# First head's projection ahead of half of the values, rotary tables by transposes, and a planner with other durations and a shared port

## The chip, the core and the metric

The kernel runs on one core of a Trainium2 chip. The engines are TensorE (PE, with its weight loads shown as PEld), VectorE (DVE), ScalarE (ACT), GpSimd (POOL) and SyncE (SP, which issues most DMAs). The metric is the device time of one execution in microseconds; lower is better.

## What is computed

Two layers of a decoder on 512 tokens of width 1024. Each layer has a mixing part with two groups of heads, an output projection, and a SwiGLU FFN, with RMS norms before and after both parts.

```python
for l in range(DEPTH):                      # DEPTH = 2
    h = rms_norm(x, attn_pre_g[l])
    qa, ka, va, qb, kb, vb, f_logit = jnp.split(h @ w_in[l], split_at, axis=-1)
    qa = partial_rotary(qa.reshape(b, s, 2 * N_HEADS_DIFF, HEAD_DIM), cos, sin)
    ka = partial_rotary(ka.reshape(b, s, 2 * N_HEADS_DIFF, HEAD_DIM), cos, sin)
    ...
    oa = diff_attention(qa, ka, va, lam)    # 4 heads, softmax 0 minus lam times softmax 1
    oa = rms_norm(oa, diff_sub_g[l]) * (1.0 - lam_init)
    ob = forgetting_attention(qb, kb, vb, log_sigmoid(f_logit + forget_bias[l]))   # 8 heads
    x = x + rms_norm(jnp.concatenate([oa, ob], -1) @ w_out[l], attn_post_g[l])
    h = rms_norm(x, ffn_pre_g[l])
    y = (jax.nn.silu(h @ w_gate[l]) * (h @ w_up[l])) @ w_down[l]
    x = x + rms_norm(y, ffn_post_g[l])
```

The rotary part turns the first 16 of each head's 64 columns by angles position times frequency.

## The kernel before, in words

Activations lie transposed (`hT_h`, `hT_l`: 128 columns by 8 blocks by 512 tokens). Every fp32 product is made of three matmuls: each operand is split into a rounded part and a rest (`_h` or `wh`, written by ACT; `_l` or `wl`, the difference, written by DVE or POOL), and high times high, high times low and low times high are summed in PSUM.

The attention part of a layer is not written in its order. Functions (`start`, `tables`, `tile_chunk`, `v_chunks`, `diff_head`, `fox_head`, `o0_chunk`, `o1_chunks`) add operations to a `Plan`: engine, a duration in ns (from `dV`, `dA`, `dG` of the number of columns, or a constant), operations that it depends on, a key (lower goes first among those that are ready) and the buffers that it takes and gives. `Plan.run` walks through planned time and emits each engine's instructions in the order that comes out; that order is then fixed, and on the chip each engine executes its own list and waits on semaphores. Operations with a key from `FILLER` on are fillers: PE takes them when nothing else is ready by the plan.

In layer 0, `start` loads x and the weights of the diff heads' values (`w_load`, 4 chunks `c`), normalizes the four blocks of 128 tokens, transposes them (`hp_a`), and makes the values `va` (4 token blocks `t` by 4 chunks, 6 matmuls each). Matmuls on zeros (from `sinT`) keep PE busy until then. `tables` makes the rotary tables: SP loads the positions eight times, DVE reduces 32 angles per partition, ACT takes the sines, and the tables go through DRAM (`tab_d`) into `cosT` and `sinT`. It also loads the mask, the matrix of ones (`tu`, cast into `upr`) and the small parameters (`lv`, `fbb`, `dsg`). Then fillers follow each other: key and query projections of a pair of heads (`pj_kd`, `pj_qd`, `pj_kf`, `pj_qf`, 24 matmuls each), values of the other group (`vb`), output projection (`o`). A diff head needs rotated queries and keys (`t1`, `t2` on DVE, then splits), scores (`sd`), softmax on DVE and ACT (`ed`; L958 is the combination of the two softmaxes), transposes (`ptd`) and its product with the values (`od`). A fox head has a bias made by POOL, scores `sf`, softmax (`ae`; L1037 scales by the row sums), transposes `ptf` and the product `of`. Weights of most projections are split with the rest on POOL (`wl_` in L649).

In layer 1 the values are made at the end of layer 0's FFN, and its plan starts at the key projection. The FFN is outside the plan.

## Time and profile before

| | us |
|---|---|
| runs of the kernel before | 1246.26 median of 3 (1244.06 to 1253.99) |
| profiled execution | 1249.71 |
| its span in the trace | 1247.9, mean granted clock 0.993 |
| PE busy in the span | 1201.7 (96%) |
| DVE, ACT, POOL busy | 817.3 (65%), 599.2 (48%), 210.4 (17%) |

The profiled execution is 3.45 us above the median, and 1.8 us of it lie around the span. A busy PE is not PE at its peak: a matmul's record runs on after the next has started, so short gaps between matmuls do not show as idle time.

### The profile page before, as it was taken

Reading aid. Unit: us, or ns where it says so; the run is one execution under the profiler, and the core shown is the slowest. Engines: PE = TensorE matmul, PEld = TensorE weight load, DVE = VectorE, ACT = ScalarE, POOL = GpSimd, SP = SyncE. Lnnn points to the kernel's source line nnn. Section 1 sums busy time; section 2 is a strip of 40 time slices with the busy share of each in tenths; the row PEclk is TensorE's granted clock in tenths of the full one; section 3 lists DMA queues with packets and bytes.
Section 4 is the critical chain, followed back from the end, with each engine's and each line's share of the span. In section 5 each row is a group of like instructions: output and inputs, shape, how many; then the busy total and the mean of one; then the engine's idle time right before and its main releaser. Section 6 shows DMA issues by size and latency. Waiting matters only on the chain.

```text
span 1247.9 us, 16724 instructions
## 1 busy us (share of the span) xinstructions
PE 1201.7 (96%) x5817; PEld 989.3 (79%) x5817; DVE 817.3 (65%) x1574; ACT 599.2 (48%) x1162; POOL 210.4 (17%) x250
## 2 busy tenths in 40 slices
PE   8999999999999999999799999999999999999996
PEld 5787877788888888887687878777988888887875
DVE  7697858665554545576848977695755455555855
ACT  5476757553333233365544767674533233324643
POOL 1302457320000000000223124572200000000001
PEclk9999999999999999999999999999999999999999
DMA  7333443416575766798504333434167676677863
GB/s 231 91 85 93 112 115 105 136 37 196 188 238 182 227 203 211 251 313 264 171 2 119 90 89 93 121 110 125 62 192 242 196 214 212 208 233 247 294 203 125
DMA packets 211268, 206.75 MB, mean 166 GB/s; under 512 B 11680, under 2 KB 155680, under 8 KB 211184
## 3 DMA queue, kind: packets, MB, share of 16 engines
q1 hardware_dynamic: 211040, 205.16, 53.2%
q8 instruction: 46, 0.75, 0.3%
q10 hardware_dynamic: 144, 0.52, 0.1%
q14 instruction: 38, 0.31, 0.1%
HBM read 163.34 MB, written 33.91 MB: 158 GB/s over the span
## 4 chain that ended last, share of the span: by engine, by line
PE 44%; issue 32%; DVE 13%; ACT 4%; DMA 4%; POOL 2%; SPq 0%; POOLq 0%; DVEq 0%; ACTq 0%
PE pj_g L205 10%; PE pj_u L205 10%; PE o L205 4%; PE va L205 3%; PE pj_kf L205 2%; PE pj_kd L205 2%; PE da L205 2%; PE pj_qf L205 2%; DMA rs<-s_d 2%; PE vb L205 1%; DVE t2kd L739 1%; PE db L205 1%; PE ptf L210 1%; DVE ed L958 1%; PE of L205 1%
## 5 line engine op out<-in xcount | busy, mean ns | idle before, releaser
L205 PE MATMUL pj_g<-hT_h,wh_g 128*128 128x512 f32 (+1 forms) x384 | 142.9, 372 | 0.0
L205 PE MATMUL pj_g<-hT_l,wh_g 128*128 128x512 f32 (+1 forms) x384 | 142.6, 371 | 0.0
L205 PE MATMUL pj_g<-hT_h,wl_g 128*128 128x512 f32 (+1 forms) x384 | 142.6, 371 | 0.0
L205 PE MATMUL pj_u<-hT_h,wh_u 128*128 128x512 f32 (+1 forms) x368 | 140.1, 381 | 0.0
L205 PE MATMUL pj_u<-hT_l,wh_u 128*128 128x512 f32 (+1 forms) x368 | 139.8, 380 | 0.0
L205 PE MATMUL pj_u<-hT_h,wl_u 128*128 128x512 f32 (+1 forms) x368 | 139.8, 380 | 0.0
L271 POOL TENSOR_SCALAR v_fp<-s_fp 128x1 f32<-128x1 f32 x8 | 5.2, 651 | 685.4 <-ACT junk L277 354.7
L259 DVE TENSOR_TENSOR wl_u<-wr_u,wh_u 128x1024 fp32r<-128x1024 f32 x44 | 53.9, 1225 | 98.5 <-ACT wh_u L258 98.5
L258 ACT CAST wh_g<-wr_g 128x1024 fp32r<-128x1024 f32 x44 | 46.4, 1054 | 145.9 <-PE pj_u L205 86.9
L205 PE MATMUL da<-wh_d,op 128*128 128x512 f32 x352 | 111.3, 392 | 2.1 <-ACT wh_d L258 2.1
L258 ACT CAST wh_u<-wr_u 128x1024 fp32r<-128x1024 f32 x44 | 46.3, 1053 | 135.4 <-PE pj_g L205 128.3
L1239 DVE TENSOR_TENSOR sg<-pj_u,sg 128x512 f32<-128x512 f32 x44 | 30.4, 690 | 80.8 <-PE pj_u L205 80.8
L205 PEld LDWEIGHTS pj_g<-hT_h,wh_g 128*128 128x128 f32 x384 | 72.4, 188 | 12.7
L205 PEld LDWEIGHTS pj_g<-hT_h,wl_g 128*128 128x128 f32 x384 | 72.2, 188 | 12.5
L205 PEld LDWEIGHTS pj_g<-hT_l,wh_g 128*128 128x128 f32 x384 | 72.3, 188 | 12.3
L205 PE MATMUL da<-wl_d,op 128*128 128x512 f32 x176 | 69.7, 396 | 10.9 <-DVE wl_d L259 10.9
L205 PEld LDWEIGHTS pj_u<-hT_h,wl_u 128*128 128x128 f32 x368 | 69.2, 188 | 13.2
L205 PEld LDWEIGHTS pj_u<-hT_h,wh_u 128*128 128x128 f32 x368 | 69.2, 188 | 13.1
L205 PEld LDWEIGHTS pj_u<-hT_l,wh_u 128*128 128x128 f32 x368 | 69.2, 188 | 12.9
L205 PEld LDWEIGHTS da<-wh_d,op 128*128 128x128 f32 x352 | 66.4, 189 | 16.4 <-ACT wh_d L258 2.9
L258 ACT CAST wh_d<-wr_d 128x1024 fp32r<-128x1024 f32 x42 | 44.2, 1052 | 42.4 <-PE da L205 15.4
L259 DVE TENSOR_TENSOR wl_d<-wr_d,wh_d 128x1024 fp32r<-128x1024 f32 x42 | 51.3, 1222 | 19.2 <-ACT wh_d L258 18.6
(301 smaller groups left out, 3019.1 us busy)
## 6 DMA issues: line engine op xcount, KB each, us to landing
wr_g<-in_w_gate_dram SPq DMA_DIRECT2D x44, 512.0 KB, 4.4
wr_u<-in_w_up_dram SPq DMA_DIRECT2D x44, 512.0 KB, 4.6
b<-in_w_down_dram SPq DMA_DIRECT2D x88, 256.0 KB, 3.6
t_d<-b SPq DMA_DIRECT2D x88, 256.0 KB, 4.0
wr_d<-t_d SPq DMA_DIRECT2D x24, 512.0 KB, 4.9
wr_d<-in_w_down_dram SPq DMA_DIRECT2D x18, 512.0 KB, 5.0
wr_o<-in_w_out_dram SPq DMA_DIRECT2D x16, 512.0 KB, 4.4
xr<-t_d SPq DMA_DIRECT2D x16, 512.0 KB, 5.1
```

The costliest lines, as they stand in the source:

```text
L205: ins = PE.matmul(out, a, b, start=start, stop=stop)
L210: ins = PE.transpose(out, a, idn)
L258: A.copy(hi, raw)
L259: (eng or V).tensor_sub(lo, raw, hi.bitcast(F32))
L271: G.tensor_scalar(v, s2[:, 0:1], scalar1=s2[:, 1:2], scalar2=EPS, op0=ALU.add, op1=ALU.add)
L739: return V.tensor_mul(b["t2"], b["t2"], sinT)
L958: return V.scalar_tensor_tensor(e0, e0, b["r"][:, 0:1], e1, op0=ALU.mult, op1=ALU.add)
L1239: V.tensor_mul(sg, pu, sg)
```

## The change

Six things are edited, all in the attention part.

1. In layer 0 the values of token blocks 2 and 3 get a filler's key (`VA_EARLY` = 2), and the first diff head's key and query projections a key ahead of them. For this, the value weights get other buffers, so that those of keys and queries are free.
2. The rotary tables: one DMA from ACT's queue loads the positions as 128 partitions by 4 elements; DVE makes angles for 8 frequencies and reduces them, in `start`, with a key near those of the norms; ACT writes sines and cosines into two tiles of 128 tokens by 4 blocks; PE transposes these, and ACT copies the results into `cosT` and `sinT`. The way through DRAM is gone. ACT loads the table set for sines first of all.
3. The planner's durations: `dV`, `dA`, `dG` and several constants are larger.
4. The planner gets a port: POOL's operations and the DVE operations with `port=True` don't overlap in planned time.
5. The rest of the weights of the first half of the output projection (`o0_chunk`) is made by DVE in place of POOL, four chunks in each layer.
6. The zeros for the first matmuls come from `upr`, and `mixed_d` is allocated later.

```diff
-TB = S // 16
-VA_C, VA_T = 4, 1
+VA_C, VA_T, VA_EARLY = 4, 1, 2
...
+        self.port = port or eng == "G"
...
+        port = {"V": 0.0, "G": 0.0}
...
+                        if o.port:
+                            r = max(r, port["G" if e == "V" else "V"])
...
+            if o.port:
+                port[o.eng] = start + o.dur
...
-                return 68 + 1.04 * n
+                return 110 + 1.05 * n
 
             def dA(n):
-                return 60 + 0.83 * n
+                return 115 + 0.83 * n
 
             def dG(n):
-                return 120 + 2.15 * n
+                return 180 + 2.17 * n
...
-                plan.free.update(g=[], v8=[0.0], qs=[], ks=[])
+                plan.free.update(g=[], v8=[], rc=[], rd=[], pt=[])
+                tc.keep_in_program_order(A.preload_act_table_set("trig_and_small"))
...
-                idd = dma(con[:, :P], con_d[:, :P], P)
+                idd.append(dma(con[:, :P], con_d[:, :P], P))
+                rotary()
...
-                    raw = (mixed_d, raw_v)[c // 2][:, 2 * (c % 2):2 * (c % 2) + 2]
-                    if c == 0:
-                        dst = q_tile("wva0h"), q_tile("wva0l")
-                    elif c < 3:
-                        w = k_tile(f"wva{c}")
-                        dst = w[:, 0], w[:, 1]
+
+                    lo = (wv_l0, wv_l1)[c // 2][:, 2 * (c % 2):2 * (c % 2) + 2]
+                    if c < 2:
+                        hi = wv_h0[:, 2 * c:2 * c + 2]
                     else:
-                        dst = [wpool.tile([P, WCH], F32R, name=f"{x}_va3", tag=x).rearrange("p (a b) -> p a b", a=2)
-                               for x in ("wh", "wl")]
-                    hi, lo = dst
+                        x = ("wh", "wl")[c - 2]
+                        hi = wpool.tile([P, WCH], F32R, name=f"{x}_va", tag=x).rearrange("p (a b) -> p a b", a=2)
+                    tag = "pt" + "hl"[c % 2]
+                    raw = ap.tile([P, 10 * P], F32, name=f"rawv{c}", tag=tag, bufs=2)[:, :WCH]
+                    raw = raw.rearrange("p (a b) -> p a b", a=2)
...
-                                         key=500 + VA_C * c + VA_T * t)
+                                         key=(500 if t < VA_EARLY else FILLER - 20) + VA_C * c + VA_T * t)
...
+                def mix():
+                    nonlocal mixed_d
+                    mixed_d = ap.tile([P, NDIFF, S], F32, name=f"mixd{l}", tag="v8", bufs=5)
...
+                mix_op.append(add("P", 0, mix, half, key=-99, take=["v8"], order="v8"))
...
+                w = rbuf("rd", F32, "rot")
+                tabs = [rbuf("rc", F32, n) for n in ("rcos", "rsin")]
...
+                v = op("A", 500, lambda: A.dma_start(pos, pos_d[0].rearrange("(j p) -> p j", p=P)), [], lat=3000)
+                v = op("V", 80, lambda: V.tensor_copy(pf, pos), [v])
+                v = op("V", 700, lambda: [lambda f=f, c=c: V.tensor_scalar_mul(an[:, f * NT:(f + 1) * NT], pf, c)
+                                          for f, c in enumerate(_inv_freq())], [v])
...
+                    src = (nn, an)[z].rearrange("p (f j) -> p j f", j=NT)
+                    if z == 0:
+                        return lambda: A.activation(out, src, AF.Sin, bias=halfpi, scale=-1.0)
+                    return lambda: A.activation(out, src, AF.Sin, scale=1.0 if half else -1.0)
...
+                    a = op("A", 800, lambda z=z: [place(z, half, m) for half in range(2) for m in range(2)], [dep])
+
+                    def tr(z=z):
+                        x[z] = (bank_t, bank_s)[z](f"rot{z}")
+                        for j in range(NT):
+                            transpose(x[z][:, j * P:(j + 1) * P], tabs[z][:, j * P:(j + 1) * P], ident)
+                    p = op("P", 436, tr, [a, idd[0]], take=["ts"[z]])
+                    ends.append(op("A", dA(S), lambda z=z: A.copy((cosT, sinT)[z], x[z]), [p], give=["ts"[z]]))
+                add("A", 0, lambda: None, ends, key=-99, give=["rc", "rc", "rd"])
+                tab.extend(ends)
...
+                def sums():
+                    x["tu"] = rbuf("rc", F32, "tu")
+                    return nc.sync.dma_start(x["tu"], con_d[:, C_U:C_U + S])
+                tab.append(add("Q", 1.43 * S, lambda: nc.sync.dma_start(con[:, P:], con_d[:, P:NKEEP]), key=1, lat=2000,
+                               order="ld"))
+                du = add("Q", 1.43 * S, sums, key=1, lat=2000, order="ld rc", take=["rc"])
+                p = op("A", 1300, lambda: A.preload_act_table_set("natural_log_exp_and_others"), last + tab)
                 tab.append(p)
                 tab.append(op("V", 340, lambda: V.tensor_copy(upr, x["tu"]), [du] + last, give=["rc"]))
...
-                                give=["wr"])
+                                give=["wr"], port=True)
...
-                last_tile[:] = fillers([(650, piece(k)) for k in range(KT)], [ready], take={0: ["g"]}, give=["w"])
+                last_tile[:] = fillers([(650, piece(k)) for k in range(KT)], [ready], take={0: ["g"]}, give=["w"],
+                                       key=FILLER - 40 if kind == "d" and l == z == 0 else FILLER)
...
-                        e = add(eng, d, lo(m), [a], key=key, give=give if m else [])
+                        e = add(eng, d, lo(m), [a], key=key, give=give if m else [], port=kind == "d")
...
-                v3 = add("V", dV(S), t2, [v2], key=key)
-                g1 = add("V", dV(S), t3, [v3], key=key, give=["rd"])
+                v3 = add("V", dV(S), t2, [v2], key=key, port=True)
+                g1 = add("V", dV(S), t3, [v3], key=key, give=["rd"], port=True)
...
-                v = add("V", dV(n), top, [o], key=n_key, give=["s"])
-                return b, add("A", 282 + 0.83 * n, expo, [v], key=n_key)
+                v = add("V", dV(n)+80, top, [o], key=n_key, give=["s"])
+                return b, add("A", 370 + 0.87 * n, expo, [v], key=n_key)
...
-                    v = add("V", 75, inv, [a], key=nk)
-                    v = add("V", 70 + 0.65 * n, norm, [v], key=nk)
+                    v = add("V", 110, inv, [a], key=nk)
+                    v = add("V", 185 + 0.5 * n, norm, [v], key=nk, port=True)
...
                 box, ready = load(wout_d[l][kc * P:(kc + 2) * P, :S].rearrange("(k p) n -> p k n", p=P), [P, 2, S],
-                                  f"o0{l}{kc}")
+                                  f"o0{l}{kc}", eng=V)
```

Order on PE in layer 0 around the first scores of diff head 0 (`sd0000`, `sd0001`); `kd01` and `qd01` are the projections for head 1, `va02` and `va03` the values of token blocks 2 and 3. Before:

```order
L205 MATMUL pj_kd01_542<-hT_h_79,wl_kd01_464 128x512
L205 MATMUL pj_qd01_585<-hT_h_79,wh_qd01_496 128x512
L205 MATMUL pj_qd01_585<-hT_l_80,wh_qd01_496 128x512
L205 MATMUL pj_qd01_585<-hT_h_79,wl_qd01_497 128x512
L205 MATMUL sd0000_591<-ksd0_0_522,qsd0_0_566 128x128 x2
L205 MATMUL sd0001_594<-ksd0_0_522,qsd0_0_566 128x128 x2
```

Now:

```order
L214 MATMUL va03_121<-wl_va_116,hT_l_80 128x512
L214 MATMUL pj_kd01_569<-hT_h_79,wh_kd01_466 128x512
L214 MATMUL pj_kd01_569<-hT_l_80,wh_kd01_466 128x512
L214 MATMUL pj_kd01_569<-hT_h_79,wl_kd01_467 128x512
L214 MATMUL sd0000_573<-ksd0_0_503,qsd0_0_553 128x128 x2
L214 MATMUL sd0001_576<-ksd0_0_503,qsd0_0_553 128x128 x2
```

Between head 0's query projection and its first scores stood 24 matmuls of kd01 and 3 of qd01; now 36 of va02 and va03 and 3 of kd01 stand there.

Order on DVE at the start of layer 0, from the square sum of the first token block (`ISA`) on; `rot` are the angles, `h_a` the normalized block. Before:

```order
L472 ISA ss_a_116 128x1
L487 SCALAR_TENSOR_TENSOR h_a_162<-xs,r_s_117,g_apre_105 128x512
L487 SCALAR_TENSOR_TENSOR h_a_153<-xs,r_s_117,g_apre_105 128x512
L428 TENSOR_TENSOR wva0l_107<-mixd_101,wva0h_106 128x512 x2
L502 TENSOR_TENSOR hT_l<-hp_a_169,hT_h 128x4x128
```

Now:

```order
L486 ISA ss_a_122 128x1
L559 CAST rot_107<-rot_107 128x4
L560 TENSOR_SCALAR rot_107<-rot_107 128x4 x8
L563 TENSOR_SCALAR rot_107<-rot_107 128x32
L501 SCALAR_TENSOR_TENSOR h_a_178<-xs,r_s_123,g_apre_106 128x512
L565 TENSOR_SCALAR rot_107<-rot_107 128x32
L501 SCALAR_TENSOR_TENSOR h_a_159<-xs,r_s_123,g_apre_106 128x512
L568 SCALAR_TENSOR_TENSOR rot_107<-rot_107 128x32
```

The cast, which needs the loaded positions, stands ahead of the first norm, and the other steps of the angles between the norms and splits that follow.

Order on SP after the last chunk of the value weights; `wr_kd00` and `wr_qd00` are the weights of head 0's projections. Before:

```order
L545 DMA rot_0_234<-in_positions_dram 16x32 x8
L536 DMA con_81<-in_constants_dram 128x513
L536 DMA tu_0_281<-in_constants_dram 128x512
L637 DMA wr_kd00_297<-in_w_in_dram 128x8x128
L637 DMA wr_qd00_308<-in_w_in_dram 128x8x128
L589 DMA lv_325<-in_lam_q1_dram 128x64
```

Now:

```order
L617 DMA lv_263<-in_lam_k2_dram 128x64
L619 DMA fbb_89<-in_forget_bias_dram 128x8
L620 DMA dsg_90<-in_diff_sub_g_dram 128x1
L604 DMA tu_0_369<-in_constants_dram 128x512
L665 DMA wr_kd00_384<-in_w_in_dram 128x8x128
L665 DMA wr_qd00_394<-in_w_in_dram 128x8x128
```

The weights stood behind the positions; now they stand behind the small parameters and `tu`, and `tu` takes a buffer of the rotary tables, so its load waits until PE has transposed them.

## Rows read from the trace of the kernel before

**Rows 1.** The page: the chain that ended last, by engine.

```profile
PE 44%; issue 32%; DVE 13%; ACT 4%; DMA 4%; POOL 2%; SPq 0%; POOLq 0%; DVEq 0%; ACTq 0%
```

**Rows 2.** Four stretches: us, busy (xcount) of PE, PEld, DVE, ACT, POOL; clock; DMA.

```profile
77.10:104.60 27.50, 24.42 (x157) 21.40 (x156) 26.09 (x77) 23.06 (x60) 7.17 (x3) 0.97 0.37 97
695.40:723.20 27.80, 24.71 (x158) 21.66 (x157) 26.29 (x78) 23.34 (x61) 7.19 (x3) 0.96 0.36 96
100.00:105.00 5.00, 3.17 (x10) 2.33 (x10) 4.86 (x22) 5.00 (x16) 2.38 (x1) 0.79 0.11 28
230.00:235.00 5.00, 3.12 (x11) 2.27 (x10) 4.68 (x11) 2.74 (x8) 1.90 (x1) 0.76 0.76 224
```

**Rows 3.** Timeline of PE, start us and us: first products.

```profile
20.72 1.03 PE L210 MATMUL hp_a<-con,h_a 128*128 128x128 f32 x8
...
37.93 0.39 PE L205 MATMUL pj_kd<-hT_h,wh_kd 128*128 128x512 f32 x1
...
43.37 0.39 PE L205 MATMUL pj_qd<-hT_h,wh_qd 128*128 128x512 f32 x1
```

**Rows 4.** Timeline of PE: first scores, [idle before], and first FFN matmul.

```profile
55.77 0.41 PE L205 MATMUL sd<-ksd,qsd 128*128 128x128 f32 x2 [0.68 <-issue]
...
60.08 0.62 PE L205 MATMUL sd<-ksd,qsd 128*128 128x384 f32 x2 [0.58 <-DVE md L875]
...
270.57 0.28 PE L205 MATMUL pj_g<-hT_h,wh_g 128*128 128x256 f32 x1
```

**Rows 5.** Timeline of DVE: two operations on SBUF operands.

```profile
44.95 2.50 DVE L739 TENSOR_TENSOR t2kd<-t2kd,sinT 128x512 f32<-128x512 f32 x1
...
229.75 2.23 DVE L1037 TENSOR_SCALAR ae<-ae,lf 128x128 f32<-128x128 f32 x1
```

**Rows 6.** Timeline of POOL in the same two places.

```profile
44.52 2.39 POOL L649 TENSOR_TENSOR wl_qd<-wr_qd,wh_qd 128x1024 fp32r<-128x1024 f32 x1 [2.83 <-ACT wh_qd L645]
...
229.55 2.35 POOL L649 TENSOR_TENSOR wo1l<-wr_o,wo1h 128x1024 fp32r<-128x1024 f32 x1
```

**Rows 7.** DVE by line and form, 38 to 271 us: busy us, mean ns.

```profile
L739 DVE TENSOR_TENSOR t2kd<-t2kd,sinT 128x512 f32<-128x512 f32 x4 | 7.3, 1822 | 0.1
...
L1037 DVE TENSOR_SCALAR ae<-ae,lf 128x128 f32<-128x128 f32 x8 | 5.6, 695 | 0.1
...
L742 DVE TENSOR_TENSOR t1kd<-t1kd,t2kd 128x512 f32<-128x512 f32 x4 | 2.8, 688 | 0.1
```

**Rows 8.** POOL by line and form, 38 to 271 us.

```profile
L649 POOL TENSOR_TENSOR wl_o<-wr_o,wh_o 128x1024 fp32r<-128x1024 f32 x4 | 10.1, 2524 | 5.8 <-ACT wh_o L645 5.8
```

**Rows 9.** Timeline of PE: three waits.

```profile
100.83 0.41 PE L210 MATMUL ptd<-con,ed 128*128 128x128 f32 x2 [0.73 <-DVE lg L782]
102.34 0.50 PE L205 MATMUL pj_kd<-hT_h,wh_kd 128*128 128x512 f32 x1 [1.10 <-DVE vf L795]
...
232.13 0.30 PE L210 MATMUL ptf<-con,ae 128*128 128x128 f32 x1 [1.88 <-DVE ae L1037]
```

**Rows 10.** The start: timelines of ACT, SP, DVE; two DMA issue rows.

```profile
0.72 0.41 ACTq L407 DMA_DIRECT2D g_apre<-in_attn_pre_g_dram  x1
1.16 1.28 ACT L468 ACT_TABLE_LOAD   x1 [1.16 <-PEq L1429]
...
7.03 9.30 SPq L545 DMA_DIRECT2D rot<-in_positions_dram  x8
...
6.87 0.08 DVE L472 DVE_READ_ACCUMULATOR2_ANT ss_a<- 128x1 f32 x1
8.13 1.42 DVE L487 SCALAR_TENSOR_TENSOR h_a<-xs,r_s,g_apre 128x512 f32<-128x512 f32 x2 [1.18 <-POOL r_s L395]
...
27.87 0.64 DVE L563 SCALAR_TENSOR_TENSOR rot<-rot 128x32 f32<-128x32 f32 x3
...
rot<-in_positions_dram SPq DMA_DIRECT2D x8, 2.0 KB, 5.4
...
dsg<-in_diff_sub_g_dram SPq DMA_DIRECT2D x2, 0.5 KB, 3.6
```

More of the change, by code (lines that the diff above doesn't have):

```diff
@@ L76, in __init__, with add @@
         self.margin, self.ops, self.last, self.idle = margin, [], {}, None
-    def add(self, eng, dur, fn, deps=(), key=0.0, take=(), give=(), lat=0.0, order="", ready=0.0):
-        o = Op(eng, dur, fn, deps, key, take, give, lat)
+    def add(self, eng, dur, fn, deps=(), key=0.0, take=(), give=(), lat=0.0, order="", ready=0.0, port=False):
+        o = Op(eng, dur, fn, deps, key, take, give, lat, port)
         o.ready = ready
@@ L521, in start @@
-                add("P", 0, lambda: None, wl[2] + wl[3], key=-99, give=["v8"])
+                def mix():
+                    nonlocal mixed_d
+                    mixed_d = ap.tile([P, NDIFF, S], F32, name=f"mixd{l}", tag="v8", bufs=5)
+                add("P", 0, lambda: None, sum(wl.values(), []), key=-99, give=["pt", "pt"])
+                half, full = ([done[t, c] for t in range(NT)] for c in (1, 3))
+                add("P", 0, lambda: None, half, key=-99, give=["v8", "v8"])
+                add("P", 0, lambda: None, full, key=-99, give=["v8", "w"])
@@ L1002, in diff_head @@
                     mixed_d[:, h], mixed_d[:, h], dsg[:, l:l + 1], b["nrm"], op0=ALU.mult, op1=ALU.mult), [a, c],
-                    key=key + LAG_SS, give=["e"])]
+                    key=key + LAG_SS, give=["e"], port=True)]
             def fox_head(hh, n0):
```

111 lines of the change are left out of this document (46 added, 65 removed).

## The prediction

> **What bounds the kernel now.** I read the chain of waits first, then PE's timeline through layer 0's attention, then what DVE and POOL do where PE waits. The chain is PE 44%, issue 32%, DVE 13% [rows 1]: PE sets the time, and DVE is the only other engine with a real share. So I count how much of the attention part PE does not fill. A projection of 24 matmuls of 512 columns runs from 37.93 to 43.37 us [rows 3], 0.227 us each; other widths I take in proportion, and a 128-column transpose at 0.11 us (eight take 1.03 us with the tail of the last [rows 3]). From the first score at 55.77 to the first FFN matmul at 270.57 [rows 4] are 214.8 us. By the order PE has there 571 matmuls of 512 columns, 96 of 264, 158 of 256, 62 of 384, 62 of 128 and 140 transposes: 129.6 + 11.2 + 17.9 + 10.5 + 3.5 + 15.4 = 188 us. **About 27 us are unfilled** in layer 0, and layer 1 has the same order and much the same times: the stretch between the value products of diff heads 0 and 1 takes 27.5 us in layer 0 and 27.8 us in layer 1 [rows 2]. The FFN has the same instructions in the same order after the change, so only this slack and the start can move.
>
> Where the slack comes from shows in that stretch. PE's work in it is 22 x 0.227 + 96 x 0.117 + 11 x 0.170 + 7 x 0.113 + 7 x 0.057 + 13 x 0.11 = 21 us of 27.5, while DVE is busy 26.1 of 27.5 [rows 2]. But DVE is not at work all that time. The product of two SBUF tiles L739 takes 2.50 us at 44.95, when POOL's subtraction runs from 44.52 for 2.39 us; the scaling L1037 takes 2.23 us at 229.75 beside POOL's 2.35 us from 229.55 [rows 5, 6]. In both places DVE's record ends just after POOL's. Four L739 average 1822 ns, where the next operation on the same tiles, L742, of the same shape and also in SBUF alone, averages 688 [rows 7]: 4 x 1.13 = 4.5 us lost on this one line, and L1037 on 128 columns averages as much as that operation on 512. So DVE stands blocked while POOL works, with other work behind it in its list. PE then waits 0.73 and 1.10 us at 100.83 and 102.34, and 1.88 us at 232.13 for the 2.23 us operation [rows 9]. After such waits the granted clock falls to the lower of its two levels (1.2 in place of 2.4 GHz) for a while: 0.79 in the slice from 100 and 0.76 from 230 [rows 2], which costs 1.05 and 1.2 us in these slices.
>
> **The change part by part.** (The sum is made against the profiled execution, 1249.7 us, and carried over to the median, 1246.3, which is 3.45 us lower.)
>
> *Rotary tables, start of layer 0.* Removed: eight position loads that hold SP for 9.30 us from 7.03 [rows 10], the four loads of the tables and their way through DRAM. In the trace those were hidden behind the values. Added, ahead of everything: the cast of the positions stands on DVE before the first norm, so the whole start waits for the one position load. ACT loads its table first (1.28 us), then issues the gains (0.41 us) where the gains were first before [rows 10]; the position load is issued near 0.7 + 1.3 + 0.4 = 2.4 us. It has 512 pieces of four bytes. The nearest rows: a small parameter, 128 such pieces, lands 3.6 us after issue; a position load of 16 pieces in the crowded start takes 5.4 us [rows 10]. Lowest bound 2.4 + 3.6 = 6.0, which is before DVE is free at 6.95: no wait. Highest, if time grew with the pieces, 2.4 + 4 x 3.6 = 16.8 us. I take the 5.4 us plus one for the pieces, about 8.8 us, since the crowd and not the count made that row long. Ahead of the norm come then 10 small operations: about 1 us, as three of 32 columns take 0.64 us one after the other [rows 10]. The norm starts near 9.9 in place of 8.13 [rows 10], and 16 more small operations follow between the norms, at 0.1 (overlapped) to 0.21 us each, 1.6 to 3.4 us, of which I count 0.5 as late. Together +2 us (0 to +9), and the eight transposes for the tables add 0.9 us to PE. By the Trainium skill, "DMA: Bandwidth & Descriptors", section "Queues, rings and completion order", a DMA engine turns between queues by whole packets of some 9 to 17 descriptors; by that rule the position load would land soon after the gains, and this +2 would be 0. No row here shows it.
>
> *Head 0's projections ahead.* No work is added. The weights of head 0 are now issued behind the small parameters and behind `tu`, which waits for PE's transposes of the tables; I expect that at 22 to 24 us, the load takes about 5 us, and ACT's and DVE's splits some 2.3, so the weights are there near 31, about when PE comes to them (60 of 96 value matmuls, 13.6 us, 40 transposes). I cost this at nothing; the cover is thin, and each us of delay there is a us of PE, because its list has no other work at that place. The gain: between the end of head 0's query projection and its scores stand 39 matmuls (8.9 us) in place of 27 (6.1 us). The scores came 55.77 - 48.81 = 7.0 us after that projection (its end is 43.37 + 24 x 0.227 = 48.81), so the waits of 0.68 and 0.58 us [rows 4] go: -1.3 us. Layer 1's order too has more PE work ahead of its first scores, another -1.3 us. That scores stand 24 matmuls earlier in layer 0 is worth no more by itself; it moves 5.4 us of filler to where PE waits.
>
> *Durations and port.* With both, the planner puts DVE operations that don't need the port beside POOL's, and spreads fillers. By the new order PE has 25.8 us of work between the value products of heads 0 and 1 in layer 0 (21 before), against about 24 us of DVE operations at unblocked durations. Of the 6.5 us of slack in this stretch I take 3.5 back, the dip of the clock with it; in layer 1, where the new order has 19.6 us of PE work against 19.5 of DVE's, 3. Bounds: 0 (the waits move) and 6.5 each. *Fox heads:* the wait at 232.13 and the slow clock after it are 1.9 + 1.2 us, and the four splits of `o0_chunk` that leave POOL (10.1 us, 2524 ns each [rows 8]) no longer hold up the biases and DVE. I take -4 in layer 0 and -2 in layer 1, where the dip is missing (bounds 0 and -8 together per layer). PE's work left after the last fox product falls from 29.4 to 23.3 us in both layers: fillers have moved forward into the gaps, which is what the gain consists of if the gaps are still there.
>
> *`o0_chunk` on DVE.* Four more DVE operations per layer of about 1.2 us (twice the 0.6 us pitch of 512 columns). The last two fox heads follow each other with 7.8 and 5.3 us of PE work, and DVE has as much to do per head; I count +1 in layer 0 and +1.5 in layer 1 for new waits (0 to +5 together).
>
> *Sum:* +2 + 0.9 - 1.3 - 1.3 - 3.5 - 3 - 4 - 2 + 1 + 1.5 = **-9.7 us**, that is 1240.0 for the profiled execution's state and **1236.6** on the median's. By the skill's rule above the sum would be 1234.6.
>
> **The rivals.**
> - *The plan does not hold on the chip* (the change doesn't do what it says). An order is fixed, durations vary, and DVE and POOL meet on the port at other places. For it: the order before came from a planner too and was off by 27 us a layer. Against: its blocked operations were systematic, POOL's 2.4 us ones. Then only the first-score waits and the start count: +2.9 - 2.6 = 0.3, 1246.6; with a little of the rest 1243 to 1250.
> - *More comes back.* PE waits once too often everywhere in layer 0; if half of the 27 us of each layer goes, it is -27 + 2.9 = -24: 1222. For it: the dips of the clock, the waits of rows 9 and DVE's blocked time have one cause. Against: the many short handovers stay.
> - *Slower: the position load is late.* It lands at 16.8; the norm starts near 18, nearly 10 us late, of which some 9 stay, since PE has nothing else. Behind it the tables, `tu` and head 0's weights come later by the same amount. With the first-score gain and the extra DVE work: +9 + 0.9 - 2.6 + 2.5 = +9.8, 1256, if the planner's gain of 12.5 does not come as well. It decides from a landing about 12 us on, when the start loses more than half of that gain. For it: the pieces of four bytes, and a whole engine behind one cast. Against: the rows of 3.6 and 5.4 us.
>
> **How the numbers follow.** Forecast 0.48 (1230 to 1243), no plan effect 0.27, more back 0.17, slower 0.08. The likeliest time is 1236.6. The range reaches from the middle of the larger gain to the upper side of the no-effect case: 1224 to 1251. A measurement of this kernel can tell about 1% (12.5 us) from no change. Faster by over 1% (below 1233.8): all of "more back" and a third of the forecast, 0.33. Slower by over 1% (above 1258.7): half of the slower case, 0.04. Within 1%: 0.63.
>
> **What the profile of the changed kernel would show.** The first norm on DVE starts between 8 and 11 us. The first `sd` starts near 52 to 53 us without idle time ahead of it. The first FFN matmul starts near 264 in place of 270.57. L739 averages under 1.2 us and L1037 on 128 columns under 0.5; the granted clock has fewer dips in attention. POOL has no `wl_o` of this half. I would be wrong if the first norm starts after 12 us, if PE waits at head 0's key projection for its weights, or if L739 and L1037 stay as long as now.

## The result, and the profile after

The changed kernel takes 1242.56 us (median of 15 runs) against 1248.32 us for the kernel before on the same chip: a ratio of 0.995, 95% interval 0.9934 to 0.9967. It is about 0.5% faster, less than the 1% that the prediction set for "faster"; 1236.6 was forecast, in a range of 1224 to 1251. One of the 15 runs took 2413.32 us; there is no trace of it, and the ratio leaves it out. The profiled executions are 1249.7 us before and 1242.1 us after, 7.6 us apart, and the account below is made between these two.

The start first: PE's first transposes, DVE's first work with the positions and its first norm, the issue and the landing of the position load (last column of the DMA row).

```profile
8.94 0.66 PE L219 MATMUL hp_a<-con,h_a 128*128 128x128 f32 x4 [1.95 <-DVE h_a L501]
...
51.25 0.34 PE L214 MATMUL sd<-ksd,qsd 128*128 128x128 f32 x2
51.81 0.41 PE L214 MATMUL sd<-ksd,qsd 128*128 128x128 f32 x2 [0.23 <-DMA ksd<-ksd]
```

```profile
6.80 0.17 DVE L559 CAST rot<-rot 128x4 f32<-128x4 int32 x1
...
8.13 0.75 DVE L501 SCALAR_TENSOR_TENSOR h_a<-xs,r_s,g_apre 128x512 f32<-128x512 f32 x1 [0.25 <-POOL r_s L405]
```

```profile
0.72 1.28 ACT L412 ACT_TABLE_LOAD   x1 [0.72 <-PEq L1458]
...
1.19 0.45 ACTq L558 DMA_DIRECT2D rot<-in_positions_dram  x1
```

```profile
rot<-in_positions_dram ACTq DMA_DIRECT2D x1, 2.0 KB, 5.2
```

The norm starts at 8.13 us as before [rows 10]; the positions, issued at 1.19 us, landed 5.2 us later, at 6.4, before DVE had finished its first square sum (6.87). The scores come 4.5 us earlier, with 0.23 us of waiting in place of the 0.68 and 0.58 of [rows 4].

The chain that ended last, by engine (page), answers to [rows 1]; DVE's share has gone from 13% to 5%:

```profile
PE 58%; issue 31%; DVE 5%; POOL 2%; DMA 2%; ACT 2%; SPq 0%; POOLq 0%; DVEq 0%; ACTq 0%
```

The first two stretches of this view (us, busy and count of each engine, granted clock, DMA) are those of [rows 2], from the value product `od` of head 0 to that of head 1, in layer 0 and in layer 1. The third is the one from the sixth to the seventh fox product `of` in layer 1.

```profile
71.90:99.60 27.70, 26.89 (x182) 24.66 (x181) 24.21 (x76) 22.41 (x56) 7.43 (x3) 1.00 0.41 106
691.10:718.50 27.40, 23.76 (x140) 21.14 (x141) 21.57 (x71) 20.52 (x53) 7.17 (x3) 0.88 0.37 97
837.30:850.70 13.40, 8.81 (x41) 6.73 (x39) 8.02 (x19) 5.86 (x12) 0.00 (x0) 0.87 0.55 157
```

In layer 0 PE now has more work there and the clock holds at 1.00. In layer 1 nothing is gained and the clock is at 0.88. The third stretch was no term of the prediction: PE is busy 8.81 of its 13.40 us.

VectorE by line and form, 38 to 260 us (busy us, mean ns), answers to [rows 7]:

```profile
L978 DVE TENSOR_TENSOR ld<-ld,nlam 128x1 f32<-128x1 f32 x16 | 6.0, 376 | 0.6
...
L767 DVE TENSOR_TENSOR t2kd<-t2kd,sinT 128x512 f32<-128x512 f32 x4 | 4.5, 1127 | 0.1
...
L1066 DVE TENSOR_SCALAR ae<-ae,lf 128x128 f32<-128x128 f32 x8 | 2.7, 339 | 0.0
```

L739 (now L767) has gone from 1822 to 1127 ns and L1037 (now L1066) from 695 to 339. But a product of one column, L978, averages 376 ns, where the smallest is 159. Its mean was 162 ns before. Three of the 16 take 1.12 to 1.35 us here, each until GpSimd's split beside it ends.

For the account I take, for each stretch, its length less PE's work in it, worked out much as in the prediction: matmuls by the order, 0.227 us for 512 columns at the full clock, a transpose 0.108, and the rest in proportion, but 0.119 and 0.122 us for 256 and 264 columns, which is how they follow each other in the traces. By this the prediction's 27 us for layer 0 are 25.5. This is **unfilled** time. For the kernels below:

| kernel | us, median | ratio to before, 95% interval | start | att. 0 | FFN 0 | att. 1 | FFN 1 |
|---|---|---|---|---|---|---|---|
| before | 1246.9 to 1248.3 | 1 | 13.5 | 25.5 | 11.9 | 25.4 | 6.0 |
| after (the change) | 1242.6 | 0.9950 (0.9934 to 0.9967) | 13.6 | 12.9 | 14.0 | 28.8 | 4.9 |
| ffn_casts_behind | 1229.0 | 0.9857 (0.9835 to 0.9879) | 13.4 | 9.2 | 11.4 | 22.7 | 4.4 |
| before_casts_behind | 1247.9 | 0.9991 (0.9968 to 1.0014) | 14.2 | 25.5 | 12.7 | 23.6 | 4.5 |
| start_alone | 1247.2 | 0.9998 (0.9978 to 1.0019) | 15.8 | 18.3 | 15.2 | 23.8 | 6.0 |
| port_ignored | 1253.6 | 1.0053 (1.0033 to 1.0072) | 15.4 | 26.4 | 14.8 | 26.3 | 5.9 |
| casts_port_ignored | 1256.2 | 1.0059 (1.0036 to 1.0083) | 15.5 | 27.7 | 15.1 | 26.9 | 4.1 |
| casts_values_first | 1242.3 | 0.9973 (0.9953 to 0.9994) | 13.9 | 19.9 | 11.9 | 22.7 | 4.4 |
| casts_o0_on_gpsimd | 1240.4 | 0.9930 (0.9905 to 0.9956) | 13.5 | 17.8 | 14.0 | 23.8 | 4.6 |
| port_marked | 1238.3 | 0.9932 (0.9910 to 0.9953) | 13.6 | 17.7 | 13.4 | 22.7 | 4.3 |
| casts_port_marked | 1231.9 | 0.9887 (0.9855 to 0.9919) | 13.3 | 12.5 | 12.4 | 20.8 | 5.0 |
| casts_margin60 | 1232.2 | 0.9883 (0.9851 to 0.9914) | 13.4 | 9.3 | 13.7 | 22.1 | 5.2 |
| casts_ld_on_scalar | 1231.7 | 0.9884 (0.9853 to 0.9916) | 13.5 | 13.7 | 12.7 | 17.2 | 3.2 |
| casts_ld_scalar_layer1 | 1227.3 | 0.9828 (0.9802 to 0.9854) | 13.9 | 10.6 | 13.9 | 17.2 | 2.8 |

(start: to the first score of layer 0; att. 0: from there to the FFN's first matmul; FFN 0: to the first values of layer 1; att. 1: from there to the FFN; FFN 1: to the last matmul. One profiled execution each.)

The kernels below the second row were run in three groups, each beside the kernel before, whose median there is 1246.9 to 1247.1 us, against 1248.3 beside the changed kernel. A difference to the changed kernel's median carries these 1.2 to 1.4 us: the 13.5 us of the next section are 11.6 by the ratios and 13.1 by the profiled spans.

So layer 0's attention gains 12.6 us of unfilled time, layer 1's loses 3.4, layer 0's FFN loses 2.1 with the same matmuls in the same order, layer 1's FFN gains 1.1, and 0.9 us of transposes are added.

### The profile page after: what moved, and what is told of

Read it like the earlier page. It is cut to its first block, busy times and chain, and to the rows that moved or that the text cites. A ratio compares the mean times of both kernels' runs of the same rounds, so it can differ in the third digit from the quotient of the medians.

```text
span 1240.3 us, 16748 instructions
## 1 busy us (share of the span) xinstructions
PE 1199.6 (97%) x5826; PEld 995.1 (80%) x5826; DVE 808.7 (65%) x1588; ACT 600.3 (48%) x1168; POOL 195.5 (16%) x243
## 4 chain that ended last, share of the span: by engine, by line
PE 58%; issue 31%; DVE 5%; POOL 2%; DMA 2%; ACT 2%; SPq 0%; POOLq 0%; DVEq 0%; ACTq 0%
PE pj_g L214 10%; PE pj_u L214 10%; PE vb L214 4%; PE da L214 4%; PE pj_kd L214 4%; PE pj_qd L214 4%; PE pj_kf L214 4%; PE pj_qf L214 3%; PE o L214 3%; PE db L214 2%; PE va L214 2%; PE sd L214 1%; PE of L214 1%; PE sf L214 1%; PE od L214 1%
## 5 line engine op out<-in xcount | busy, mean ns | idle before, releaser
L214 PE MATMUL da<-wh_d,op 128*128 128x512 f32 x352 | 114.3, 402 | 1.2 <-ACT wh_d L266 1.2
L214 PEld LDWEIGHTS pj_g<-hT_h,wl_g 128*128 128x128 f32 x384 | 72.3, 188 | 12.6
L214 PEld LDWEIGHTS pj_g<-hT_h,wh_g 128*128 128x128 f32 x384 | 72.3, 188 | 12.6
L214 PEld LDWEIGHTS pj_g<-hT_l,wh_g 128*128 128x128 f32 x384 | 72.2, 188 | 12.5
L214 PEld LDWEIGHTS pj_u<-hT_h,wl_u 128*128 128x128 f32 x368 | 69.1, 188 | 13.1
```

The costliest lines, as they stand in the source:

```text
L214: ins = PE.matmul(out, a, b, start=start, stop=stop)
```

## The experiments

**The FFN's first casts in the fox heads' tail.** ScalarE in layer 1 of the changed kernel, where the third stretch lies (start us, us; idle time before and its releaser in brackets):

```profile
837.05 0.62 ACT L914 ACTIVATE ae<-ae,mf 128x384 f32<-128x384 f32 x1
837.57 0.19 ACT L914 ACTIVATION_READ_ACCUMULATOR ae<-ae,mf 128x1 f32 x1
841.15 1.05 ACT L266 CAST wh_g<-wr_g 128x1024 fp32r<-128x1024 f32 x1 [3.39 <-DMA wr_g<-in_w_gate_dram]
842.10 0.72 ACT L914 ACTIVATE ae<-ae,mf 128x512 f32<-128x512 f32 x1
842.73 0.19 ACT L914 ACTIVATION_READ_ACCUMULATOR ae<-ae,mf 128x1 f32 x1
842.94 0.58 ACT L1090 COPY mixf<-of 64x512 f32<-64x512 f32 x1
843.54 1.04 ACT L266 CAST wh_u<-wr_u 128x1024 fp32r<-128x1024 f32 x1
```

and PE there:

```profile
845.33 0.66 PE L219 MATMUL ptf<-con,ae 128*128 128x128 f32 x4 [3.52 <-DVE mixf L1092]
847.06 0.47 PE L219 MATMUL ptf<-con,ae 128*128 128x128 f32 x1 [1.07 <-DVE ptlf L951]
```

ScalarE is free at 837.76 and stands for 3.39 us for the gate weights of the FFN, which are used only from 880 us on. The exp of a fox head and the copy of `of` are queued behind that cast. PE then waits 3.52 us for `mixf`. Before the change this cast came after the last exp and waited for nothing:

```profile
851.93 0.72 ACT L886 ACTIVATE ae<-ae,mf 128x512 f32<-128x512 f32 x1 [1.40 <-DVE mf L875]
852.56 0.19 ACT L886 ACTIVATION_READ_ACCUMULATOR ae<-ae,mf 128x1 f32 x1
852.77 0.37 ACT L919 CAST pthf<-ptf 128x256 fp32r<-128x256 f32 x1
853.04 1.06 ACT L258 CAST wh_g<-wr_g 128x1024 fp32r<-128x1024 f32 x1
```

The plan does not contain these casts; they are placed behind it, by when the weights' buffer comes free. The edit loads the first gate and up weights right behind the plan and keeps their casts there:

```diff
+    late = lambda i, name: tc.keep_in_program_order(i) if name in ("g00", "u00", "g10", "u10") else i
...
-        A.copy(hi, raw)
+        late(A.copy(hi, raw), name)
...
-        wh, wl = load_w(src_w[:, col:col + P].rearrange("(k p) n -> p k n", p=P), [P, KT, P], name)
+        wh, wl = ahead.pop(name, None) or load_w(src_w[:, col:col + P].rearrange("(k p) n -> p k n", p=P), [P, KT, P], name)
...
             plan.run(tc.keep_in_program_order, first)
+            for x, w in (("g", wg_d[l]), ("u", wu_d[l])): ahead[f"{x}{l}0"] = load_w(w[:, :P].rearrange("(k p) n -> p k n", p=P), [P, KT, P], f"{x}{l}0")
```

> The changed kernel with one thing more: the casts of the FFN's first gate and up weights stand on ScalarE behind the last of attention, instead of among the last fox heads; TensorE's and GpSimd's orders are the same. Theory A (ScalarE stands 3.39 us before the gate weights have landed, with a fox head's exps queued behind it, and TensorE pays for that): in layer 1 the stretch from the sixth to the seventh of's first matmul falls from 13.4 us to 7 to 9 us, in layer 0 from 11.6 to 8 to 9 us, the clock dip near 846 goes, and the time is 1233 to 1237 us, 6 to 9 under the changed kernel's 1242.6. Theory B (these stretches are short of something else, the vectors' chain of the fox heads, and the wait only lies beside it): the stretches stay within 1.5 us of what they were and the time is 1241 to 1244 us.

1229.0 us, 13.5 under the changed kernel (11.6 by the ratios): theory A, and more than it gave. The stretch in layer 1 falls from 13.4 to 7.1 us, that in layer 0 from 11.6 to 8.2. With the casts behind, the exp follows on at once:

```profile
831.99 0.73 ACT L914 ACTIVATE ae<-ae,mf 128x512 f32<-128x512 f32 x1 [0.49 <-DVE mf L903]
832.62 0.18 ACT L914 ACTIVATION_READ_ACCUMULATOR ae<-ae,mf 128x1 f32 x1
832.83 0.58 ACT L1090 COPY mixf<-of 64x512 f32<-64x512 f32 x1
...
846.99 1.04 ACT L266 CAST wh_g<-wr_g 128x1024 fp32r<-128x1024 f32 x1
```

```profile
831.00:838.20 7.20, 7.20 (x41) 5.89 (x39) 5.86 (x17) 3.71 (x10) 0.00 (x0) 1.00 0.89 277
```

Most of the rest is layer 0's FFN, 362.0 to 359.4 us, of which more in the last section.

> The kernel before the change with the FFN's first casts behind the last of attention. There no exp of the fox heads stands behind them. Theory A (the casts hurt only where they stand ahead of exps, which the change brought about): within 1.5 us of the kernel before. Theory B (casts and splits among the last transposes and copies cost something already there, and the gain of 13.5 us on the changed kernel is not all owed to the change): 3 to 6 us under the kernel before, from layer 0's last two fox stretches and layer 1's.

1247.9 us, ratio 0.9991: theory A. In the kernel before the edit is worth nothing, so the loss came in with the change.

**The parts of the change, each taken back.** `start_alone` has the new start with all the old durations, `port` ignored and the o weights on GpSimd (the next two diffs); of the durations, for instance:

```diff
-                return 110 + 1.05 * n
+                return 68 + 1.04 * n
```

> Only the start of the change: rotary tables by transposes and the first head projected ahead of half of the values, with the durations of before, no port rule, and the o weights split on GpSimd as before. Theory A (the start and the planner share layer 0's 11.7 us): first scores near 51 us (55.8 before), layer 0's FFN begins near 264 to 266 us, layer 1's attention takes 256 us as before, and the time is 1242 to 1245 us. Theory B (the start gains nothing that the attention does not give back, and the planner carries all): the FFN begins within 2 us of 270.6 us and the time is 1247 to 1250 us. Theory C (the start carries all of layer 0 and the planner's part is a loss in layer 1): the FFN begins by 260 us and the time is 1236 to 1240 us.

Theory A for the places, if only just (266.5 lies outside its 264 to 266), B for the time. The scores come at 50.06 us and the FFN begins at 266.5 instead of 270.6, but the FFN then takes 363.1 us instead of 359.9, and 1247.2 us cannot be told from before.

```diff
-                        if o.port:
+                        if False:
                             r = max(r, port["G" if e == "V" else "V"])
```

> The changed kernel with the plan's rule on the shared port left out (measured durations, the o weights on VectorE and the new start stay). Theory A (the port rule is what took the long waits out of the diff heads): the t2kd product with sinT is back at a mean of 1.4 us or more in both layers, the fox heads' 128-column normalization at 0.45 us or more, and the time is 1246 to 1250 us. Theory B (the durations and the o weights on VectorE do it, the rule adds nothing): the time is 1240 to 1244 us.

> The kernel with the FFN casts behind attention (1229.0 us), with the plan's rule on the shared port left out. Theory A (the rule itself is worth the 11 us that it was worth without the cast edit): 1238 to 1242 us, with diff heads in layer 0 (first to second od) at 36 us or more. Theory B (without the rule the list merely happened to put the casts at a worse place): 1229 to 1233 us, with the last two fox stretches of each layer back at 6 to 9 us.

1253.6 and 1256.2 us: the rule is worth 11 us in the changed kernel, and 27 us once the casts are out of the way. For the first, theory A had the direction, and its 1246 to 1250 was too low. Of its signs only one came: the product with `sinT` averages 1761 ns in layer 0, but 1134 in layer 1, and the 128-column scaling 331. For the second, theory A had the direction again, but its 1238 to 1242 missed: without the rule the cast edit gains nothing. In `port_ignored` there was little to gain, for the gate cast stands ahead of one exp only and waits for no load (at 234.06 and 851.11 us). What holds up the last fox stretches there is the port: VectorE's scaling of 512 columns stands beside GpSimd's split, and PE waits behind it. One row each of VectorE, GpSimd and PE in that kernel:

```profile
228.87 2.46 DVE L1066 TENSOR_SCALAR ae<-ae,lf 128x512 f32<-128x512 f32 x1
```

```profile
228.67 2.38 POOL L677 TENSOR_TENSOR wo1l<-wr_o,wo1h 128x1024 fp32r<-128x1024 f32 x1 [2.88 <-ACT wo1h L673]
```

```profile
232.10 1.18 PE L219 MATMUL ptf<-con,ae 128*128 128x128 f32 x7 [2.08 <-DVE mixf L1092]
```

The same scaling, L1066 on 512 columns, averages 998 ns in layer 0 of `port_ignored` and 493 in the changed kernel.

```diff
-                                  f"o0{l}{kc}", eng=V)
+                                  f"o0{l}{kc}")
```

> The kernel with the FFN casts behind attention, with the first half's o weights split on GpSimd as before the change. Theory A (the move took 2.5 us instructions off the engine that also makes the fox heads' biases, and it is worth some us in the fox heads): the fox stretches of a layer, first to last of, are 2 to 4 us longer in each, and the time is 1233 to 1237 us. Theory B (VectorE pays for the move what GpSimd saves): 1227.5 to 1231 us. Theory C (the move costs more on VectorE than it saves): 1222 to 1227 us.

1240.4 us, 11.4 more: theory A in layer 0, with a larger price than it gave; in layer 1 the fox heads are only 0.4 us longer, where it gave 2 to 4. Most of it is one stretch of layer 0, from the fifth to the sixth `of`, which has 8.3 us unfilled (0.4 with the o weights on VectorE). PE waits 5.91 us, from 206.60 on, and VectorE is held up twice ahead of what it waits for: the split of `mixf` takes 2.87 us (0.68 the next time), and three scalings 3.45 us, each beside a split on GpSimd:

```profile
205.33 2.87 DVE L1100 TENSOR_TENSOR hT_l<-mixf,hT_h 128x512 fp32r<-128x512 f32 x1
...
209.80 3.45 DVE L1066 TENSOR_SCALAR ae<-ae,lf 128x512 f32<-128x512 f32 x3
```

```profile
204.91 2.74 POOL L677 TENSOR_TENSOR wo1l<-wr_o,wo1h 128x1024 fp32r<-128x1024 f32 x1 [0.25 <-ACT wo1h L673]
...
209.30 2.78 POOL L677 TENSOR_TENSOR wl_o<-wr_o,wh_o 128x1024 fp32r<-128x1024 f32 x1
```

```profile
212.51 1.30 PE L219 MATMUL ptf<-con,ae 128*128 128x128 f32 x5 [5.91 <-DVE ae L1066]
```

```diff
-VA_C, VA_T, VA_EARLY = 4, 1, 2
+VA_C, VA_T, VA_EARLY = 4, 1, 4
...
-                                       key=FILLER - 40 if kind == "d" and l == z == 0 else FILLER)
+                                       key=FILLER)
```

> The kernel with the FFN casts behind attention, but with all of layer 0's first values projected ahead of the first head, as before the change (tables by transposes and the planner's part stay). Theory A (the first head's early projection is worth its 4 us of earlier scores to the end): first scores near 55 to 56 us, layer 0's FFN begins 3 to 5 us later than at 255.1, and the time is 1231.5 to 1234 us. Theory B (the values are owed in any case and the attention stretch behind takes the difference up): the FFN begins within 1.5 us of 255.1, and the time is 1228 to 1231 us.

1242.3 us, 13.3 more, and the FFN begins 11.1 us later: theory A, three times its size. This list is not the order of before: 48 matmuls of head 1's projections stand ahead of the first scores, where 27 stood before, and the scores come at 61.76 us, not at the 55 to 56 that the theory had. So the 13.3 us are the price of the list that the plan makes without leftover values. The loss does not lie ahead of the scores. It lies behind them, where PE lacks filler: from the first score to the first `od` 5.0 us are unfilled instead of 0.6, from `od` 0 to `od` 1 6.5 instead of 1.8. From there on layer 0's stretches agree with those of layer 1, which never has values left over.

**The port again, in layer 1.** PE's longest wait in attention of the changed kernel beside those of the casts, with VectorE and GpSimd at the same time:

```profile
710.64 0.77 PE L214 MATMUL pj_kd<-hT_h,wh_kd 128*128 128x512 f32 x1 [3.29 <-DVE vf L823]
```

```profile
707.48 1.63 DVE L978 TENSOR_TENSOR ld<-ld,nlam 128x1 f32<-128x1 f32 x1
```

```profile
706.75 2.35 POOL L677 TENSOR_TENSOR wl_kf<-wr_kf,wh_kf 128x1024 fp32r<-128x1024 f32 x1 [1.66 <-ACT wh_kf L673]
```

A product of 128x1 takes 1.63 us, until GpSimd is done at 709.10. ScalarE's scaling of `ed` needs it, and the casts of `vf`, for which PE waits, stand behind that scaling:

```profile
709.21 0.40 ACT L982 ACTIVATE ed<-ed,ld 128x128 f32<-128x128 f32 x1 [1.17 <-DVE az L842]
```

The product is held up for 1.47 us (1.63 less 0.16), less than half of PE's 3.29. In layer 0 it is held up three times, by 0.96 to 1.19 us, and PE has only 1.8 us unfilled there: what it costs depends on the filler that PE has left. The plan marks as users of the port only some of VectorE's steps, and this product is not among them. `port_marked` marks it and the split of `mixf`:

```diff
-                    v = add("V", 250, rl, [x[0][1], x[1][1]], key=key)
+                    v = add("V", 250, rl, [x[0][1], x[1][1]], key=key, port=True)
...
-                           give=["v8"] if k == NDIFF - 1 else [])
+                           give=["v8"] if k == NDIFF - 1 else [], port=True)
```

> The changed kernel with the plan told that two more of VectorE's steps wait for GpSimd: the reciprocal with its 128x1 product (ld), and the split of the fox halves of o's operand (hT_l from mixf). Theory A (the stalls that the new plan leaves in layer 1 come from steps that it does not know to wait): the 128x1 product falls from a mean of 376 ns in layer 0 and 252 ns in layer 1 to under 200 ns in both, TensorE's 3.29 us wait for vf near 710 us is gone, od0 to od1 in layer 1 falls from 27.4 to under 24 us, and the time is 1236 to 1240 us. Theory B (such stalls are scattered over the plan whatever it knows, and a new list only moves them): the product gets shorter but another wait of 2 to 4 us shows up in its place, and the time is 1240 to 1246 us.

> The kernel with the FFN casts behind attention and the two further steps marked as users of the shared port. Theory A (marking them is worth what it gave in layer 1, and layer 0's loss of 4.8 us in the run without the cast edit came in part from the casts): 1222 to 1227 us. Theory B (the marks moved stalls, with a gain only because the casts did less harm there): 1228 to 1232 us, with layer 0's od0 to od1 again at 33 to 34 us (27.7 without).

The product falls to 178 ns in layer 0 and 161 in layer 1, and the time is in A's range (its interval overlaps that of the changed kernel), but the wait for `vf` stays, 3.22 us: theory B. With the casts out of the way the marks are worth nothing (1231.9 against 1229.0, intervals overlapping), and layer 0's `od` 0 to 1 takes 33.9 us as B said. There PE waits 2.86 us for `vf` too, and no operation beside that wait is lengthened: ScalarE has the cast of the next weights (1.04 us) and two scalings (1.01 us) ahead of the casts of `vf`. The port is not the only reason for such waits. Another step that the plan does not mark has taken the product's place, the first of the forget gates' chain, 128x32, which takes 0.18 us when free. In layer 1 of `port_marked` it takes 1.86 us. So it does in the run with a margin of 60, where nothing was marked:

```profile
703.22 1.97 DVE L842 SCALAR_TENSOR_TENSOR az<-lg 128x32 f32<-128x32 f32 x1
```

```profile
702.79 2.36 POOL L677 TENSOR_TENSOR wl_kf<-wr_kf,wh_kf 128x1024 fp32r<-128x1024 f32 x1 [1.65 <-DVE lg L810]
```

```diff
-MARGIN, PEX, T0 = 50.0, 20.0, 10000.0
+MARGIN, PEX, T0 = 60.0, 20.0, 10000.0
```

> The kernel with the FFN casts behind attention (1229.0 us) with one number of the plan changed that stands for nothing measured: its margin for TensorE's scores and transposes is 60 instead of 50 ns. It asks how far a new list alone moves the time. Theory A (the plan holds, its lists are about equally good): within 1.5 us of 1229.0, each stretch of a layer's attention within 1 us. Theory B (stalls fall where they fall, each new list shuffles them): attention stretches move by 2 to 7 us either way, and the time is 1225 to 1236 us but outside 1227.5 to 1230.5.

The unfilled time of layer 0's attention changes by 0.1 us and that of layer 1's by 0.6, and no stretch's by more than 0.5: theory A, for attention, though one stretch is 2.3 us shorter, mostly because it has less work in it. The median is 3.2 us higher, outside A's bound, with 2.3 us of it in layer 0's FFN; the ratios' intervals overlap. This list differs in few places, though, so it does not bound what a wholly new one can do: in `casts_port_marked` and `casts_ld_on_scalar`, whose lists are new throughout, layer 0 loses 3.3 and 4.5 us. Differences of that size cannot be put down to the edit alone; those of 11 us and more are well outside.

The next two kernels take the product off VectorE:

```diff
-                        return [lambda: V.reciprocal(b["r"], b["r"]),
-                                lambda: V.tensor_mul(b["r"][:, 1:2], b["r"][:, 1:2], nlam[:, l:l + 1])]
+                        return V.reciprocal(b["r"], b["r"])
...
-                        return A.activation(e, e, AF.Copy, scale=b["r"][:, 1:2])
+                        return [lambda: A.activation(r, r, AF.Copy, scale=nlam[:, l:l + 1]), lambda: A.activation(e, e, AF.Copy, scale=r)]
```

> The kernel with the FFN casts behind attention, and the 128x1 product of 1/l with lambda on ScalarE instead of VectorE, where GpSimd cannot hold it up. Theory A (the product that VectorE could not begin for 1.6 us near 707 us held back vf and so TensorE for 3.3 us): the wait for vf in layer 1 is under 1 us, od0 to od1 there is 25 us or less (27.5), the double dip near 704 us gets shorter or goes, and the time is 1223 to 1227 us. Theory B (the next user of the port in VectorE's list takes the wait over, or ScalarE, which gets 32 more instructions, does): 1228 to 1232 us.

> The kernel with the FFN casts behind attention, and in layer 1 alone the 128x1 product of lambda on ScalarE: layer 0's list is that of the run with the casts behind (203.9 us from first scores to the FFN), layer 1's that of the run with the product on ScalarE in both layers (247.9 us from first values to the FFN, against 253.4). Theory A (a list's stalls belong to the list and come back wherever it runs): both stretches within 0.7 us of these, and the time 1223 to 1227 us, less than with either kernel. Theory B (what a layer gains, the FFN behind it or the clock takes back): the stretches hold, but layer 0's FFN, 359.4 us in the one and 360.7 in the other, or layer 1's takes 2 us or more longer, and the time is 1228 to 1231 us.

In layer 1 it is theory A: the wait for `vf` is gone, `od` 0 to 1 falls to 23.0 us, and 17.2 us are unfilled instead of 22.7. PE still waits in that place, for `ed` (from `casts_ld_scalar_layer1`):

```profile
707.02 0.90 PE L219 MATMUL ptd<-con,ed 128*128 128x128 f32 x5 [1.83 <-DVE ed L987]
```

That is 1.47 us less than the 3.30 with the casts behind, as much as the product had been held up. The lists differ in more than the product, though. The gates' step now begins just ahead of GpSimd's split and takes 0.18 us:

```profile
703.75 0.18 DVE L842 SCALAR_TENSOR_TENSOR az<-lg 128x32 f32<-128x32 f32 x1
```

```profile
703.95 2.37 POOL L677 TENSOR_TENSOR wl_kf<-wr_kf,wh_kf 128x1024 fp32r<-128x1024 f32 x1 [1.90 <-DVE az L842]
```

In layer 0 the same edit loses 4.5 us, so in both layers together the time is B's. In layer 1 alone it gives 1227.3 us, the lowest median of all. Layer 1's stretch came back as expected (247.9 us). Layer 0's was 1.4 us longer than with the casts alone and its FFN 2.5 us longer, which is theory B's part; the time lies between the two ranges. Against the casts alone the intervals of the ratios overlap (0.9802 to 0.9854, 0.9835 to 0.9879), so the step from 1229.0 to 1227.3 is not shown; against both kernels that the prediction is about it is clear.

## Why the prediction was right, step by step

The total was right: -7.6 us in the profiled executions, where -9.7 were forecast. It was right by errors of opposite sign, and so in part by luck.

*Start:* +2 was forecast for the wait on the position load, with bounds of 0 and 9; it was 0. The load took 5.2 us, as the row of 5.4 us that I leaned on, and the one microsecond added for its 512 pieces was not there. It was also issued at 1.19 us and not at 2.4: I had put the issue behind the table load, which runs from 0.72 us for 1.28. The rule cited in the prediction from the Trainium skill, "DMA: Bandwidth & Descriptors", section "Queues, rings and completion order", that a DMA engine turns between queues by whole packets, gave 0, and the trace agrees with the 0; no run here shows whether packets are the reason. The 0.9 us of transposes came as counted. Head 0's weights were no stop: VectorE is done with the first at 30.5 us, PE's key projection starts at 31.5.

*Layer 0's attention:* -7.8 forecast (-1.3, -3.5, -4, +1), -12.6 measured. To the first `od` 1.4 us of unfilled time went, from `od` 0 to `od` 1 4.5, in the fox heads 4.0 up to their last product: in size these terms held. Their mechanism held less well.

The -3.5 was put down to durations and port alone. Of 6.3 us unfilled in that stretch before, 1.8 were left; without the values left over it is 6.5 (`casts_values_first`), without the port rule 7.5 (`port_ignored`). It took both. So "worth no more by itself", for the head ahead of the values, was a term put at nothing that was not nothing: the values that are left over are filler for the first two heads, and the list without them has 10.7 us more unfilled in layer 0. With the old plan (`start_alone`) the new start gives 7.2 us of unfilled time there, 2.3 of which it loses ahead of the scores, and the FFN begins 4 us earlier, not 11.7.

The fox heads' 4.0 are what the FFN's casts left of 7.5: another 3.4 us go between the sixth and the seventh `of` when the casts stand behind. And 3.3 us went between `od` 1 and the first `of`, where I had counted nothing (0.6 came back behind the last `of`). Layer 1, which has no values left over, gains 3.2 us in the same place. There, in layer 1, 1.7 us stay unfilled in the changed kernel, 2.5 without the port rule, but 4.5 in `start_alone`, with the old durations, so most of this gain goes with the durations; in layer 0 it needs the port rule too (6.6 us without it, 5.2 before).

*Layer 1's attention:* -4.8 forecast, +3.4 measured. The 3.2 us just named were gained, but three terms failed.

The fox heads' "-2" and "+1.5" became +3.1; the stretch with the FFN's casts alone has 6.4 us unfilled, and 0.1 with the casts behind. I priced the new waits as VectorE's work and never asked what else moves when the o weights' buffers come free earlier. The loads for the FFN went from 847.7 to 837.2 us and their casts into ScalarE's list ahead of exps; this is shown by the edit that takes them out. A further +2.0 lies between the fourth and the fifth `of`, where two of VectorE's scalings, which the plan marks, meet a split on GpSimd all the same (2.82 us for the two at 813.21).

The "-3" from `od` 0 to `od` 1 became +1.1. The long blocked operations went, as in layer 0, but a small one beside GpSimd's split holds back the same chain. By the rows, that accounts for some 1.5 of the 3.29 us that PE waits for `vf`; the rest is other work ahead of it in ScalarE's and VectorE's lists, and what part of it the new durations brought stays open.

The "-1.3" ahead of the first scores became +1.9 up to the first `od`. There are 0.7 us less ahead of the scores and 2.7 more behind them, in short waits of which the longest is 0.96 us, and I could name no single cause. The list without leftover values has the same 5.0 us unfilled there in layer 0.

*"FFN: the same instructions in the same order, so only this slack and the start can move":* layer 0's FFN took 2.1 us more all the same, and layer 1's 1.1 less.

*The rivals.* "The plan does not hold" is refuted for layer 0 and half true for layer 1: operations did meet at other places. "More comes back" was there to be had in part: 1229.0 needs only the FFN's casts behind attention. "Slower" was decided by the landing, early. What I named to watch for: norm at 8.13 (8 to 11), scores at 51.25 (a little ahead of 52 to 53), L739 at 1.13 (under 1.2), L1037 at 0.34 (under 0.5). The FFN began at 258.9 where I had 264, and the dips of the clock left layer 0's attention but not layer 1's.

## What to carry to other kernels

Where one part of a kernel follows an order worked out beforehand and the next part is placed around it, look at what the next part puts into the lists of the engines that the first still needs. A cast that waits for a load can stand ahead of work that is ready. And a planner that knows of a shared resource keeps apart only the users that are marked. A step of one column counts as well, by whom it holds up and not by its own length; but marking two more bought nothing here (1231.9 against 1229.0), and in layer 1 the next unmarked step took the product's place. When a gain is smaller than forecast, account by stretch before believing the total; here -12.6 and +3.4 hid behind one number.

## What was not expected of the hardware

How long a step is held up does not go by its size. A 128x1 product took 1.63 us and a 128x32 step 1.97 us, against 0.16 and 0.18 when GpSimd was not at work. Both read two operands from SBUF, and so does GpSimd's split. The Trainium skill, "SBUF — State Buffer", section "Who interferes with whom", says that a VectorE instruction with two SBUF inputs contends with a GpSimd instruction that reads SBUF, and calls the shared port pair an exclusive lock; these rows agree. The reciprocal just ahead of the product has one operand, and inside the same split (706.75 to 709.10) it was not held up:

```profile
707.29 0.16 DVE L977 RECIPROCAL ld<-ld 128x2 f32<-128x2 f32 x1
```

The count of operands is not all, though: the fox heads' scaling of one tile by a column of scalars was held up too (2.46 us at 228.87 in `casts_port_ignored`, against a mean of 493 ns for 512 columns in layer 0 of the changed kernel).

Layer 0's FFN, with the same matmuls in the same order, took 359.4 to 363.1 us in these kernels. In the changed kernel the granted clock falls to the lower level of 1.2 GHz for 3.4 us at 566.5 and for 6.8 us at 610.8, behind PE's waits for the down weights. With the casts behind it does so only at 604.5, for 6.8 us. The stretch at the first of these waits in the two kernels:

```profile
559.30:576.30 17.00, 15.02 (x59) 11.71 (x58) 6.58 (x6) 6.66 (x9) 0.00 (x0) 0.90 0.81 257
```

```profile
555.50:572.50 17.00, 15.55 (x68) 12.34 (x67) 8.51 (x8) 7.70 (x9) 0.00 (x0) 1.00 0.82 277
```

Of the 14 kernels of the table, the six with 10.2 us at the lower level in this part took 361.7 to 363.1 us, the eight with 3.4 to 6.8 us 359.4 to 361.9. Why the same waits bring the clock down in one run and not in the other stays open. So 2 to 3 us of any difference here can be the FFN's; that this is a matter of when it begins is not shown.
